# Hybrid decoder step on one core: 22 cache copies moved as quarters behind the input projection's loads, feed-forward job tables rewritten, one tile of the last pair split by halves

## The chip, the cores and the metric

One core of one Trainium2 chip runs the whole program. The metric is the device time in microseconds (us); lower is better. The kernel before was timed three times: 886.66, 887.09 and 891.93 us, median 887.09.

## The reference

One layer of a hybrid decoder, for 512 prompt tokens and 8 sample tokens that share all weights. What it computes, cut to what matters here:

```python
u = rmsnorm(x)
qA,kA,vA, qB,kB,vB,rB,gate, gA,gB = split(u @ w_in)
oA  = dilated window attention (3 groups x 4 heads; for the sample also over the caches)
oB  = gated linear attention (4 heads, state 128 x 256 per head; for the sample a step from state_gla)
mix = sigmoid(gA) * (oA @ w_pa) + sigmoid(gB) * (oB @ w_pb);   h = x + mix @ w_o
y   = rmsnorm(h + square(relu(rmsnorm(h) @ w_up)) @ w_down)
s_aG_k = concatenate(cache_aG_k, new k)[-window:]     # likewise v, for the groups G = 1, 2, 3
```

The last line matters for the change: the caches of the sample group are outputs, each shifted by one token. The bulk of them is nothing but a copy from DRAM to DRAM, 42 MB in all: 1 MB for each of a1k and a1v, 4 MB for each of a2k and a2v, 16 MB for each of a3k and a3v.

## The kernel before, in words

**Data.** The 520 token columns (512 + 8) are worked in two halves of 260. Every float32 operand is split into a high part (rounded to fp32r) and a low part (the rest), so each weight tile of 128x128 costs three products on PE: high x high, high x low and low x high. Weights come in panels of 128 output columns. A panel of 512 KB is loaded by SP (`load`, the DMA is at L118; each such DMA is chained behind the one before), its high half is made by ACT (`act`, L159) and its low half by DVE (`add`, L162; the three-operand form is at L165).

**Order of the panels.** 58 panels of the input projection (three groups of kA, qA, vA; then rB; then for each of the four GLA heads kB, qB, vB; then the gates gA and gB), then w_pa, w_pb and w_o, all in a plain loop over k tiles (`panel_mms`, products at L304); panel i+2 is loaded while panel i is multiplied. Between the products of these panels stand the small steps of attention and GLA. One of these chains recurs below, once per GLA head: SP writes a small tile `dV` (L1060, 8 KB), loads it back spread out as `sx<-dV` (L1072), ACT scales it (L1086), further steps give `ov` (ACT, L1092), and PE multiplies that into `gsp` (L1097) in its fixed place among the products. All these DMAs stand in SP's one queue, together with the panel loads and with `sx<-in_state` (L1071).

**The feed-forward.** Four quarters of it, each with four pairs of w_up panels and, in the first three, four pairs of w_down panels: 28 pairs. A pair multiplies two panels at once with seven groups of 12 products in place of eight, P1 to P7 (`pair_mm`, L262), on sums of activations (T, f) and sums of weights. A sum of weights is built by a plain load of one tile and, on the POOL queue, a DMA that adds another tile to it (`load_sums`, L146); DVE adds a further raw tile into `s`. The table `PLAN` has one line per pair that sets the order on all three engines by hand: P1 to P7 are the products, s, h and l followed by a number are the weight jobs (a sum on DVE, the high part on ACT, the low part on DVE), letters such as t2, f2, rt, sf, st, c0, hT, lT, ht, lt are the steps on the activations; "+" means for the next pair and "-" for the one before. After the last pair, the last eight w_down panels run in a plain loop (L1545 to L1575, products at L1562) in two column halves, 280 then 240. For each panel of it SP loads a tile `h` of the residual; in the first half `h` is added on DVE for the first four panels, and from the fifth panel on ACT writes it into PSUM ahead of the products (`mps<-h`, L1559), behind the splits `lw` of the next panel.

**The copies.** `pace` (L344 to L353, the DMA is at L349) issues one 1 MB copy from POOL's queue when PE has reached the last product recorded. All 42 copies go this way: 18 between the end of the gate projections (404 us) and the start of the feed-forward, 21 behind the products P4 of pairs, one more behind P4 of the last pair, and the rest in the last loop's first half, where `pace` is called after its fourth panel and later.

**Where the copies are called in the feed-forward**

```python
if p == "P4":
    self.pace(banks["copies"])
...
b = {"copies": k % 2 or qd == 3}     # up pairs
b = {"copies": 1}                    # down pairs
```

Of the kernel before, what the change touches and what calls it, by code (L numbers as in the profile page):

```python
# [13 lines left out]
ALU = mybir.AluOpType  # L14
# [25 lines left out]
l1 h7 -x0 l7 l5 P1 -y0 -y1 P5 ca h3 h4 l3 P6 u1 l4 h2 l2 P3 +X u2 +s1 +h5 -u5 P7 +h6 -u6 +l6 P2 u3 +h1 +l5 u4 P4  # L40
l1 s2 P1 h7 h3 h2 l3 P5 ca l2 -x0 -u6 -y0 P6 u1 l7 h4 -x1 l4 P3 u2 -y1 -u5 +h1 +s1 P7 +h6 P2 u3 +h5 +s2 u4 +h3 P4
l1 h7 l3 -u5 -x0 l5 P1 h2 l6 +s1 P5 ca -y0 +h1 +l1 P6 k5 l2 -x1 l7 h4 P3 k6 -y1 -u6 +s2 l4 P7 +h6 f2 +h3 rf2 P2 t2 sf2 +l6 +h5 +l3 rt2 P4
-rf1 l5 -st2 h7 +s1 -sf1 P1 -c0 -rt1 -c3 -st1 -c1 -ht1 l7 P5 -hf1 ca +s2 h2 -lf1 -hT1 -lt1 P6 k5 -c2 h4 l2 -hT0 -lT1 P3 k6 l4 -ht2 -hT2 +h1 -lT2 P7 -lT0 +h6 -lt2 +l1 +h3 P2 t2 +h5 f2 rt2 +l3 rf2 st2 P4
# [35 lines left out]
class Build:  # L79
# [163 lines left out]
    def pair_mm(self, plan):  # L243
# [10 lines left out]
        for t in plan.split():  # L254
            n = t.lstrip("+-")
            if n[0] == "P":
# [9 lines left out]
                if p == "P4":  # L266
                    self.pace(banks["copies"])
# [9 lines left out]
    def panel_mms(self, xh, xl, m, pool=None):  # L277
# [1473 lines left out]
```

## Time and profile before

| what | value |
|---|---|
| timed runs, median of 3 | 887.09 us (886.66 to 891.93) |
| the profiled execution: its own time | 882.92 us |
| its span, first to last instruction | 880.7 us |
| PE busy (products) | 862.4 us, 98% of the span |
| DVE, ACT, POOL busy | 660.3, 484.7, 111.7 us |
| mean granted TensorE clock | 0.995 |
| DMA queues q1 (SP) and q0 (POOL) | 35.0% and 28.3% of 16 engines' span |

How to read it: the profiled execution lies 4.17 us below the median of the timed runs, and 2.2 us of its time lie outside its span. A line number is that of the kernel printed above. "idle before" is the time in which an engine waited directly ahead of an instruction, and the arrow names what ended the wait. The granted clock of 1.00 is TensorE's upper level (2.4 GHz), 0.50 its lower (1.2 GHz). The DMA share is the mean busy share of the core's 16 DMA engines; it can read above 1 where two queues' packets overlap in time.

### The profile page before, as it was taken

Reading aid. Unit: us, or ns where it says so; the run is one execution under the profiler, and the core shown is the slowest. Engines: PE = TensorE matmul, PEld = TensorE weight load, DVE = VectorE, ACT = ScalarE, POOL = GpSimd, SP = SyncE. Lnnn points to the kernel's source line nnn. Section 1 sums busy time; section 2 is a strip of 40 time slices with the busy share of each in tenths; the row PEclk is TensorE's granted clock in tenths of the full one; section 3 lists DMA queues with packets and bytes.
Section 4 is the critical chain, followed back from the end, with each engine's and each line's share of the span. In section 5 each row is a group of like instructions: output and inputs, shape, how many; then the busy total and the mean of one; then the engine's idle time right before and its main releaser. Section 6 shows DMA issues by size and latency. Waiting matters only on the chain.

```text
span 880.7 us, 19661 instructions
## 1 busy us (share of the span) xinstructions
PE 862.4 (98%) x7818; PEld 843.7 (96%) x7818; DVE 660.3 (75%) x1377; ACT 484.7 (55%) x1062; POOL 111.7 (13%) x163
## 2 busy tenths in 40 slices
PE   8999999999999999999999999999999999999896
PEld 8999999999999999999999999999999999999795
DVE  6867576776866959686855678986998999988743
ACT  7243423462635536354733457976894598458543
POOL 1111000001111212111000120111111111120000
PEclk9999999999999999999999999999999999999998
DMA  7476455334445354224599896899698879887732
GB/s 260 118 277 197 146 199 186 114 114 128 150 163 197 122 185 145 86 77 170 198 362 337 313 329 174 255 282 348 187 287 264 257 221 271 267 264 231 273 123 82
DMA packets 53474, 184.13 MB, mean 209 GB/s; under 512 B 6716, under 2 KB 13892, under 8 KB 51560
## 3 DMA queue, kind: packets, MB, share of 16 engines
q1 hardware_dynamic: 39736, 106.39, 35.0%
q0 software_dynamic: 13360, 76.01, 28.3%
q8 instruction: 61, 1.00, 0.4%
q10 hardware_dynamic: 288, 0.49, 0.2%
q14 instruction: 29, 0.24, 0.1%
HBM read 167.01 MB, written 56.30 MB: 254 GB/s over the span
## 4 chain that ended last, share of the span: by engine, by line
PE 90%; DMA 4%; DVE 3%; issue 1%; ACT 1%; SPq 0%; DVEq 0%; ACTq 0%
PE mps L304 48%; PE mps L262 28%; PE mps L1562 4%; DMA sums<-in_w_up 2%; PE mps L470 1%; PE sps L645 1%; PE lev L899 1%; PE pvp L678 1%; PE gpo L1008 1%; PE gpu L1012 1%; PE ptp L662 1%; PE vps L609 1%; DMA xr<-in_xT 1%; PE gpo L1010 1%; DMA h<-Hd 1%
## 5 line engine op out<-in xcount | busy, mean ns | idle before, releaser
L304 PE MATMUL mps<-uh,whi 128*128 128x260 f32 x896 | 255.8, 286 | 0.0
L304 PE MATMUL mps<-ul,whi 128*128 128x260 f32 x896 | 255.7, 285 | 0.0
L304 PE MATMUL mps<-uh,wlo 128*128 128x260 f32 x896 | 255.2, 285 | 0.0
L159 ACT ACTIVATE whi<-raw 128x512 fp32r<-128x512 f32 (+1 forms) x210 | 129.1, 619 | 184.6 <-PE mps L304 150.4
L162 DVE TENSOR_TENSOR wlo<-raw,whi 128x512 fp32r<-128x512 f32 (+1 forms) x210 | 141.3, 677 | 44.9 <-ACT whi L159 43.2
L304 PEld LDWEIGHTS mps<-uh,wlo 128*128 128x128 f32 x896 | 168.7, 188 | 2.1 <-issue 1.5
L304 PEld LDWEIGHTS mps<-ul,whi 128*128 128x128 f32 x896 | 168.7, 188 | 1.2 <-issue 0.3
L304 PEld LDWEIGHTS mps<-uh,whi 128*128 128x128 f32 x896 | 168.7, 188 | 1.1 <-issue 0.7
L262 PE MATMUL mps<-Th,wlo 128*128 128x260 f32 x256 | 72.3, 282 | 1.7 <-DVE wlo L162 1.7
L262 PE MATMUL mps<-Tl,whi 128*128 128x260 f32 x256 | 72.2, 282 | 0.3 <-DVE Tl L162 0.3
L262 PE MATMUL mps<-Th,whi 128*128 128x260 f32 x256 | 72.3, 283 | 0.0
L262 PE MATMUL mps<-hh,wlo 128*128 128x260 f32 x240 | 67.8, 283 | 0.5 <-DVE wlo L162 0.5
L262 PE MATMUL mps<-hl,whi 128*128 128x260 f32 x240 | 67.8, 282 | 0.0
L262 PE MATMUL mps<-hh,whi 128*128 128x260 f32 x240 | 67.6, 282 | 0.0
L262 PE MATMUL mps<-fh,whi 128*128 128x260 f32 x192 | 54.5, 284 | 0.4 <-DVE dd L162 0.4
L262 PE MATMUL mps<-fh,wlo 128*128 128x260 f32 x192 | 54.1, 282 | 0.0
L262 PE MATMUL mps<-fl,whi 128*128 128x260 f32 x192 | 54.0, 281 | 0.0
L1562 PE MATMUL mps<-fh,lw 128*128 128x280 f32 (+1 forms) x256 | 49.0, 291 | 3.6 <-ACT mps L1559 3.2
L159 ACT ACTIVATE whi<-s 128x512 fp32r<-128x512 f32 x56 | 34.3, 624 | 31.4 <-DVE s L162 16.4
L262 PEld LDWEIGHTS mps<-Th,wlo 128*128 128x128 f32 x256 | 48.2, 188 | 1.9 <-DVE wlo L162 1.9
L262 PEld LDWEIGHTS mps<-Tl,whi 128*128 128x128 f32 x256 | 48.2, 188 | 0.5 <-DVE Tl L162 0.5
L262 PEld LDWEIGHTS mps<-Th,whi 128*128 128x128 f32 x256 | 48.2, 188 | 0.1
(386 smaller groups left out, 2154.9 us busy)
## 6 DMA issues: line engine op xcount, KB each, us to landing
raw<-in_w_in SPq DMA_DIRECT2D x55, 512.0 KB, 4.5
raw<-in_w_down SPq DMA_DIRECT2D x20, 512.0 KB, 6.9
sums<-in_w_up SPq DMA_DIRECT2D x16, 512.0 KB, 5.9
sums<-in_w_up POOLq DMA_DIRECT2D x16, 512.0 KB, 6.6
raw<-in_w_up SPq DMA_DIRECT2D x16, 512.0 KB, 6.6
sums<-in_w_down SPq DMA_DIRECT2D x12, 512.0 KB, 5.0
sums<-in_w_down POOLq DMA_DIRECT2D x12, 512.0 KB, 6.0
sx<-in_state SPq DMA_DIRECT2D x8, 512.0 KB, 4.6
```

The costliest lines, as they stand in the source:

```text
L159: return self.turn("ACT", self.nc.scalar.activation(*args, **kw))
L162: return self.turn("DVE", self.nc.vector.tensor_tensor(out, a, b, op=op))
L262: mm = nc.tensor.matmul(into.get(p, x), w[:, k], u, start=(p in ("P1", "P5") and k == 0 and y == 0), stop=(k == 3 and y == 2), skip_group_ ...
L304: mm = self.nc.tensor.matmul(o[:, :HC], wt, x[:, k, j * HC:(j + 1) * HC], start=(k == 0 and n == 0), stop=(k == kt - 1 and n == 2))
L470: self.last = nc.tensor.matmul(ps[i][:, j, :HC], wt, u[:, k, j * HC:(j + 1) * HC], start=(k == 0 and n == 0), stop=(k == KT - 1 and n == 1))
L609: nc.tensor.transpose(pt[:, r * P:(r + 1) * P], vt[:, r * P:(r + 1) * P], self.c["ident"])
L645: m = nc.tensor.matmul(pss[hh][:, hp, c], Q[rows, i, b * P:(b + 1) * P], K[rows, i, ks], start=True, stop=True)
L662: nc.tensor.transpose(pt[:, hh, x], prs[hp][:, hh, x * P:(x + 1) * P], self.c["ident"])
L678: m = nc.tensor.matmul(po[64 * hh:64 * hh + 64, hp * P:(hp + 1) * P], v, pTs[hp][:, hh, x], start=(x == first), stop=(x == 1))
L899: m = self.nc.tensor.matmul(out, w, x, start=True, stop=True)
L1008: nc.tensor.matmul(po[:, :256], ST[:, c], V[:, c], start=True, stop=(c == 0))
L1562: self.last = nc.tensor.matmul(ps, w, u[:, kk, cc], start=(early and kk == 0 and x == 0), stop=(kk == KT - 1 and x == 2), skip_group_check ...
```

## The change

1. **The copies.** The last 22 copies of the list (all 16 of a3v, 6 of a3k) are cut into four quarters of 16 rows x 16 KB, 88 DMAs of 256 KB. From panel 10 of the input projection on, two quarters follow each panel load on SP's queue (L118). The calls of `pace` at P4 are gone. The other 20 copies stay on POOL: 18 at their places before the feed-forward, and two at the first two calls of `pace` in the last loop, after its fourth and fifth panel.
2. **PLAN.** All 28 lines are rewritten. What is multiplied stays; the order of the jobs of ACT and DVE differs nearly everywhere. In the first line PE's order changes too: P1 P5 P2.01 P6 P3 P7 P2.23 P4 becomes P1 P5 P6.012 P2.01 P3.0 P6.3 P3.123 P7 P2.23 P4 (the digits behind a point are k tiles).
3. **The last pair.** The tile f (sf, vf, hf, lf: square, scaling, high part, low part) is worked by column halves of 260 in place of 520, and hp4 and lp4, the split of the second half of the first last-loop panel, stand together ahead of P3.

The instructions that PE, DVE, ACT, POOL and SP issue change by 0, +2, +2, -22 and +88.

```diff
             else:
...
-                if p == "P4":
-                    self.pace(banks["copies"])
...
         if i + 2 < len(self.panels):
             self.load_panel(i + 2)
+        for q in self.quarters[:2] if i >= 10 else ():
+            self.load(*self.quarters.pop(0))
...
-        for n, z, x in (("f", f, 0), ("t", t, 4)):
-            jobs["s" + n] = func(z, z, AF.Square)
-            jobs["v" + n] = lambda z=z: self.add(z(), z(), rv, op=ALU.mult)
-            jobs.update(parts(n, z, *tile(x, everything)))
+            for h, cc in (("", everything), ("1", one), ("2", two)):
+                i = of(z, cc)
+                jobs["s" + n + h] = func(i, i, AF.Square)
+                jobs["v" + n + h] = lambda i=i, cc=cc: self.add(i(), i(), rv[:, cc], op=ALU.mult)
+                jobs.update(parts(n + h, i, *tile(x, cc)))
...
+        self.quarters = []
+        for o, i in (self.copies.pop() for x in range(22)):
+            self.quarters += [[t[:, y * t.shape[1] // 4:(y + 1) * t.shape[1] // 4] for t in (o, i)] for y in range(4)]
...
-                    b = {"copies": k % 2 or qd == 3}
+                    b = {}
...
-                    b = {"copies": 1}
+                    b = {}
```

The last line of PLAN, as an example of the table:

```diff
-h5 -rf1 l5 -sf P1 h7 -vf -hf P5 ca -lf +hp0 l3 -rt1 -rt2 P6 k5 l7 -st l4 h2 +lp0 P3 k6 -vt +hp4 l2 -ht P7 R -lt P2 t2 f2 g2 rf2 q2 P4 rf1 +lp4 ht2 sf lt2 vf g1 hf q1 lf ht1 lt1
+l5 -rf1 h4 l4 P1 h7 l3 -sf -rt1 -vf P5 ca l7 -hf +hp0 -lf P6 k5 +lp0 +hp4 -st +lp4 P3 k6 -vt h2 -ht l2 P7 R f2 -lt rf2 sf2 P2 t2 vf2 g2 hf2 q2 P4 rf1 lf2 ht2 sf1 lt2 vf1 g1 hf1 q1 lf1 ht1 lt1
```

SP's queue around the third GLA head of the sample step: the last panel loads ahead of the write of `dV`, its reading back, the next panel load and the load of the state. Before:

```order
L118 DMA raw<-in_w_in 128x1024 x4
L1060 DMA dV<-vs 8x256
L1072 DMA sx<-dV 128x1024 x2
L118 DMA raw<-in_w_in 128x1024
L1071 DMA sx<-in_state 128x4x256 x2
```

And now:

```order
L118 DMA raw<-in_w_in 128x1024
L118 DMA out_ca3v<-in_ca3v 16x4096 x2
L1060 DMA dV<-vs 8x256
L1072 DMA sx<-dV 128x1024 x2
L118 DMA raw<-in_w_in 128x1024
L118 DMA out_ca3k<-in_ca3k 16x4096 x2
L1071 DMA sx<-in_state 128x4x256 x2
```

The sequence of the old DMAs is the same; two quarters now stand directly ahead of `dV`, and two more between the next panel load and the load of the state. `sx<-dV` follows `dV` directly, as before.

DVE's queue at the end of the last pair, with the numbers of the tiles (lw is a low weight part of the first last-loop panel, P5 and P6 are parts of products that ACT has copied out, mps the PSUM banks, t the tiles from which f comes, fl the low part of f). Before:

```order
L162 TENSOR_TENSOR wlo_11057<-raw_10707,whi_11056 128x512
L162 TENSOR_TENSOR fl_7067<-t_10970,fh_7066 128x520
L162 TENSOR_TENSOR t_11107<-mps_10997,P5_11051 128x260
L162 TENSOR_TENSOR t_11109<-mps_10995,P6_11072 128x260
L165 SCALAR_TENSOR_TENSOR t_11111<-t_11107,acc_6485 128x260
L165 SCALAR_TENSOR_TENSOR t_11107<-t_11107,t_11111 128x260
L162 TENSOR_TENSOR lw_10992<-raw_10851,lw_10991 128x512
L162 TENSOR_TENSOR fl_7067<-t_11107,fh_7066 128x260
L162 TENSOR_TENSOR t_11109<-t_11109,acc_6485 128x520
L165 SCALAR_TENSOR_TENSOR t_11111<-mps_10997,acc_6485 128x260
L165 SCALAR_TENSOR_TENSOR t_11107<-mps_10997,t_11111 128x260
L162 TENSOR_TENSOR fl_7067<-t_11109,fh_7066 128x520
```

And now, from the split of that panel on:

```order
L162 TENSOR_TENSOR lw_11060<-raw_10918,lw_11059 128x512 x2
L162 TENSOR_TENSOR t_11037<-t_11037,acc_6573 128x520
L162 TENSOR_TENSOR wlo_11142<-raw_10780,whi_11141 128x512
L162 TENSOR_TENSOR t_11162<-mps_11063,P6_11138 128x260
L162 TENSOR_TENSOR fl_7155<-t_11037,fh_7154 128x520
L162 TENSOR_TENSOR t_11179<-mps_11065,P5_11120 128x260
L162 TENSOR_TENSOR t_11162<-t_11162,acc_6573 128x260
L165 SCALAR_TENSOR_TENSOR t_11182<-t_11179,acc_6573 128x260
L165 SCALAR_TENSOR_TENSOR t_11179<-t_11179,t_11182 128x260
L162 TENSOR_TENSOR fl_7155<-t_11162,fh_7154 128x260
L162 TENSOR_TENSOR fl_7155<-t_11179,fh_7154 128x260
L162 TENSOR_TENSOR t_11162<-t_11162,acc_6573 128x260
```

Both halves of the split `lw` stand seven instructions and more ahead of where the second one stood, the scaling of f (`t<-t,acc`, 520 wide before) is two instructions of 260, the first of them ahead of the part that waits for the last products, and `fl` of f follows by halves as well. Behind these rows the last loop's instructions keep their order on DVE, ACT and SP.

## Rows read from the trace of the kernel before

**Rows 1.** What PE waited for, over the whole span: line waited for, us in total, times, longest us. The lines left out belong to stages that the change does not touch.

```profile
PE mps L1562 <- ACT mps L1559: 3.2, 1, 3.2
PE mps L262 <- DVE wlo L162: 2.2, 2, 1.7
...
PE gsp L1097 <- ACT ov L1092: 0.5, 1, 0.5
PE mps L262 <- DVE dd L162: 0.4, 1, 0.4
PE mps L1562 <- ACT fh L159: 0.4, 1, 0.4
PE mps L1562 <- DVE fl L162: 0.3, 1, 0.3
PE mps L262 <- DVE Tl L162: 0.3, 1, 0.3
```

**Rows 2.** Stretches of the span by windows: window, length, busy us (and instructions) of PE, PE's weight loads, DVE, ACT and POOL, then the granted clock, the DMA share and GB/s.

```profile
80.00:430.00 350.00, 349.47 (x3586) 336.07 (x3585) 244.14 (x575) 164.92 (x375) 41.48 (x63) 1.00 0.44 148
606.00:621.00 15.00, 12.85 (x106) 12.44 (x105) 9.29 (x17) 8.72 (x19) 2.96 (x3) 1.00 0.99 309
621.00:806.00 185.00, 184.49 (x1539) 184.09 (x1538) 170.97 (x337) 131.74 (x296) 27.96 (x31) 1.00 0.86 258
```

**Rows 3.** POOL's timeline from 597 to 622 us: start, length, line, operation, tiles; in brackets the idle time before and what ended it.

```profile
600.03 1.21 POOL L146 DMA_DIRECT2D sums<-in_w_up  x1 [7.20 <-DVE dd L162]
602.35 0.52 POOL L349 DMA_DIRECT2D out_ca3k<-in_ca3k  x1 [1.11 <-PE mps L262]
606.84 1.22 POOL L146 DMA_DIRECT2D sums<-in_w_up  x1 [3.97 <-ACT dd L159]
```

**Rows 4.** The timelines of DVE and PE from 609.5 to 621 us, same columns.

```profile
610.04 0.69 DVE L162 TENSOR_TENSOR s<-sums,raw 128x512 f32<-128x512 f32 x1 [2.83 <-DMA sums<-in_w_up]
...
617.33 0.69 DVE L162 TENSOR_TENSOR s<-sums,raw 128x512 f32<-128x512 f32 x1 [2.88 <-issue]
...
620.49 0.39 PE L262 MATMUL mps<-Th,wlo 128*128 128x260 f32 x1 [1.70 <-DVE wlo L162]
```

**Rows 5.** The DMA issues of the profile page: tiles, queue, count, size of one, median us from issue to landing.

```profile
raw<-in_w_in SPq DMA_DIRECT2D x55, 512.0 KB, 4.5
...
sums<-in_w_up POOLq DMA_DIRECT2D x16, 512.0 KB, 6.6
```

**Rows 6.** The same view of the window 599 to 608 us alone.

```profile
sums<-in_w_up POOLq DMA_DIRECT2D x2, 512.0 KB, 10.2
...
out_ca3k<-in_ca3k POOLq DMA_DIRECT2D x1, 10.2
```

**Rows 7.** The same view of the whole span: the 16 copies of a3v.

```profile
out_ca3v<-in_ca3v POOLq DMA_DIRECT2D x16, 7.6
```

**Rows 8.** POOL's timeline ahead of the third late weight, and PE's row that it ended.

```profile
776.47 1.20 POOL L146 DMA_DIRECT2D sums<-in_w_up  x1 [4.68 <-DVE wlo L162]
777.21 1.00 POOL L349 DMA_DIRECT2D out_ca3v<-in_ca3v  x1
...
784.41 0.39 PE L262 MATMUL mps<-hh,wlo 128*128 128x260 f32 x1 [0.51 <-DVE wlo L162]
```

**Rows 9.** The timelines of ACT and DVE at the last pair's end.

```profile
819.44 0.64 ACT L159 ACTIVATE fh<-t 128x520 fp32r<-128x520 f32 x1 [0.77 <-DVE t L162]
...
820.12 1.03 DVE L162 TENSOR_TENSOR fl<-t,fh 128x520 fp32r<-128x520 f32 x2
```

**Rows 10.** The timelines of SP, DVE and ACT behind it, to the long wait: the residual tile and the load that the chain goes through.

```profile
822.98 2.67 SPq L118 DMA_DIRECT2D h<-Hd  x1
...
827.88 0.45 DVE L162 TENSOR_TENSOR dd<-dd,h 128x280 f32<-128x280 f32 x1 [1.52 <-DMA h<-Hd]
...
829.56 0.33 SPq L118 DMA_DIRECT2D raw<-in_w_down  x1
...
832.99 1.15 ACT L159 ACTIVATE lw<-raw 128x512 fp32r<-128x512 f32 x2 [2.06 <-DMA raw<-in_w_down]
834.04 0.39 ACT L1559 ACTIVATE mps<-h 128x280 f32<-128x280 f32 x1
```

**Rows 11.** Windows as in rows 2: 819 to 823 us, and two equal stretches behind the long wait.

```profile
819.00:823.00 4.00, 3.25 (x22) 2.67 (x21) 3.90 (x9) 3.39 (x7) 0.49 (x1) 1.00 1.22 485
...
835.20:838.60 3.40, 3.40 (x17) 3.40 (x16) 2.84 (x6) 1.09 (x3) 0.00 (x0) 0.50 0.39 81
838.60:842.00 3.40, 3.40 (x28) 3.40 (x28) 1.26 (x3) 1.36 (x4) 0.49 (x1) 1.00 1.01 354
```

**Rows 12.** What ACT waited for between 200 and 345 us (the four GLA heads), columns as in rows 1.

```profile
ACT whi L159 <- DMA raw<-in_w_in: 7.7, 3, 3.0
ACT sx L1086 <- DMA sx<-dV: 7.3, 4, 3.0
```

**Rows 13.** The timelines of SP, ACT and PE at the third head.

```profile
297.93 0.29 SPq L1060 DMA_DIRECT2D dV<-vs  x1
299.64 1.68 SPq L1072 DMA_DIRECT2D sx<-dV  x2
...
304.19 0.51 ACT L1086 ACTIVATE sx<-sx,kqs 128x256 f32<-128x256 f32 x1 [2.01 <-DMA sx<-dV]
...
306.96 0.66 PE L1097 MATMUL gsp<-ident,ov 128*128 128x128 f32 x4 [0.53 <-ACT ov L1092]
```

More of the change, by code (lines that the diff above doesn't have):

```diff
@@ L40 @@
[L40 to L43, printed above, removed]
@@ new lines @@
+h7 l6 h3 l5 P1 l3 +s1 P5 ca h2 l2 P6 u1 l7 -x0 h4 -y1 P3 +X u2 +h1 +l1 P7 +h6 l4 -u6 +s2 x0 P2 u3 +h3 -u5 +l3 +h5 P4
+--u4 h7 l6 l5 P1 h2 +s1 l7 l2 P5 ca -u6 -y0 h4 P6 u1 +h1 +l1 P3 +X u2 +s2 -x1 -y1 P7 +h6 l4 -u5 -u4 P2 u3 +h5 +h3 +l5 x0 +l6 P4
+h7 l7 P1 h2 l3 -u4 l2 P5 ca +s1 -y0 +s2 P6 u1 h4 P3 u2 -x1 -y1 P7 +h6 l4 +h5 P2 u3 +h1 +l5 -u6 x1 +l1 P4
+--u5 l6 h3 -x0 -u5 P1 -y0 l3 -y1 P5 ca h7 h2 l7 P6 k5 +s1 h4 l2 P3 k6 +s2 -u6 l4 +h1 -u4 P7 +h6 f2 rf2 +l6 +h3 P2 t2 +h5 rt2 +l5 sf2 st2 +l1 P4
+h7 -c0 -rf1 l3 -ht2 P1 -lt2 -rt1 +s1 -sf1 -st1 -hf1 +s2 P5 ca -c1 h4 -lf1 l7 h2 P6 k5 -c2 -ht1 -c3 +h1 l2 P3 k6 -lt1 l4 -hT2 -hT0 -hT1 -lT0 P7 f2 +h6 -lT2 rf2 -lT1 +h3 P2 t2 +h5 +l1 rt2 sf2 +l3 P4
@@ new lines @@
+-rf1 l6 -st2 -c0 -ht2 -sf1 l5 P1 -rt1 -lt2 h7 -c1 -st1 -c3 P5 ca +s1 -hT0 l7 h2 -c2 -hf1 P6 k5 +s2 -ht1 -lT0 -hT2 -lf1 h4 P3 k6 -lT2 -lt1 +h1 l4 -hT1 l2 P7 +h6 f2 -lT1 +h3 P2 t2 +h5 +l1 rt2 rf2 +l3 st2 P4
+h7 l6 -ht2 l5 -sf2 -rf1 P1 -c0 -rt1 l7 -sf1 +h1 -c1 -st1 -c3 P5 ca -c2 -ht1 +l1 h4 +s1 P6 k5 -lt2 h2 -lt1 -hf1 l2 -hT2 P3 k6 l4 -hT0 -hT1 -lT2 -lf1 P7 +h6 f2 -lT1 rf2 -lT0 sf2 P2 t2 +h5 +s2 rt2 st2 +l5 P4
+-rf1 -sf1 -hf1 -c0 -c3 -lf1 P1 -hT0 -c1 -lT0 h3 -hT1 l6 P5 ca -lT1 -rt1 h7 l3 -st1 P6 u1 -ht2 -lt2 h2 l7 -ht1 h4 P3 u2 +h5 l2 -c2 P7 l4 -hT2 -lT2 -lt1 P2 u3 +h1 +s1 +l1 P4
@@ new lines @@
+h7 s2 h6 l5 P1 l6 h2 h3 l3 P5 ca -u4 l7 P6 u1 +h1 h4 +l1 P3 u2 l4 l2 P7 +s1 -u5 +h6 P2 u3 +h5 +s2 -u6 +h3 P4 Z
+l6 h7 -u4 l5 P1 -z l7 z0 P5 ca h2 l3 h4 P6 u1 +s1 P3 u2 -u6 l4 P7 l2 +h6 +s2 +h1 P2 u3 +h5 +l5 +l1 P4
+h7 -u4 h3 --u5 l6 P1 l3 l7 P5 ca -z1 h2 -u5 h4 P6 u1 +h1 l2 P3 u2 +s1 z0 P7 l4 -u6 P2 u3 +h5 u4 +l1 P4
+l5 h7 -u5 l7 P1 h2 s2 h6 l2 l6 P5 ca h3 h4 l3 P6 k5 +s1 -z1 P3 k6 +h5 +s2 l4 P7 +h6 +l5 +h3 +l6 P2 t2 +h1 f2 rt2 -u6 st2 +l1 P4
+-rf2 -rf1 l3 -sf2 -sf1 -c0 h7 P1 +s1 -rt1 -c1 -st1 l7 h2 P5 ca l2 -ht2 -hT1 -lt2 P6 k5 -lT1 h4 -c2 -c3 -hT2 +s2 P3 k6 +h1 -lT2 l4 -hT0 -hf1 P7 f2 -ht1 +h6 -lT0 -lf1 rf2 -lt1 P2 t2 sf2 +h5 +l1 +h3 +l5 P4
@@ new lines @@
+-rf1 l6 -rt2 -sf1 l3 -st2 P1 h7 -c0 +s1 -rt1 h4 -c3 -st1 P5 ca +s2 h2 l4 -ht1 -c1 P6 k5 l2 -hf1 l7 -ht2 -hT0 -lf1 P3 k6 -lT0 +h1 -c2 -lt2 -hT1 -lt1 P7 -hT2 f2 +h6 -lT1 +h3 -lT2 P2 t2 rf2 +h5 +l1 rt2 +l3 P4
+-rf1 l6 -st2 -sf2 l5 -sf1 P1 -c0 h7 +s1 -rt1 -c3 -st1 -c1 -hf1 P5 ca +s2 -hT1 l7 h2 P6 k5 -lf1 -c2 h4 -lT1 -hT0 l4 -hT2 P3 k6 -lT0 -ht1 -ht2 l2 +h1 P7 f2 +h6 -lt2 rf2 -lT2 sf2 -lt1 P2 t2 +h5 +l1 rt2 st2 +l5 P4
+-rf1 -sf1 -hf1 -c0 -c3 -lf1 h3 P1 -hT0 -c1 -lT0 -hT1 l6 P5 ca l3 -lT1 h7 -rt1 P6 u1 -st1 -ht1 -ht2 l7 -lt2 h2 P3 u2 h4 -c2 +h1 l2 -hT2 P7 -lt1 -lT2 l4 P2 u3 +h5 +s1 +l1 P4
@@ new lines @@
+h2 -u4 h6 l5 s2 P1 l2 h3 l6 h4 P5 ca -u6 h7 -u5 l3 P6 u1 +h1 l7 -v0 P3 u2 -v1 l4 P7 +s1 u4 +h6 P2 u3 +s2 +l1 +h3 P4
+l6 h5 l5 P1 h7 -u6 l3 -u5 P5 ca l7 h2 -v0 h4 P6 u1 +h5 -v1 P3 u2 +l5 l2 P7 l4 P2 u3 +h1 +l1 +s1 P4
+h6 s2 h7 l6 P1 h2 -u5 h3 l7 P5 ca -u4 l3 -u6 P6 u1 h4 -v0 +h1 -v1 P3 u2 l4 l2 P7 +s1 +l1 P2 u3 +h5 +h6 +l5 +l6 P4
+s2 -u4 h3 P1 h7 l3 h2 -u5 P5 ca l7 h4 -v0 +s1 P6 k5 -u6 +h5 +s2 l4 P3 k6 l2 -v1 P7 +h6 f2 +l5 rf2 +h3 P2 t2 +h1 rt2 +l1 +l3 P4
+h7 l6 -rf1 l7 P1 h2 -sf -rt1 -vf P5 ca +s1 -st -hf P6 k5 -lf +s2 P3 k6 -vt l2 -ht h4 P7 -lt +h6 l4 +h1 f2 P2 t2 +h3 +l1 +h5 +l5 P4
@@ L1224, in up_pair @@
                 jobs["q" + x] = lambda cc=cc, o=o: self.stt(t()[:, cc], o(), 0.0, g()[:, cc], op0=ALU.min, op1=ALU.mult)
-                jobs.update(parts("t" + x, of(t, cc), *tile(4, cc)))
         return jobs
```

29 lines of the change are left out of this document (6 added, 23 removed).

## The prediction

> **What bounds the kernel now.** I read four views in this order: what PE waited for, the windows by stage, the timelines around the few waits, and what ACT waited for in the heads. PE is the bound: it is busy for 98% of the span, and the first view lists every wait of any size that the change can reach. They sum to 3.2 + 2.2 + 0.5 + 0.4 + 0.4 + 0.3 + 0.3 = 7.3 us [rows 1]. The number of products is unchanged, so these 7.3 us and one stretch at the lower clock are all that can be won in the profiled execution; anything beyond must come from what the timed runs have and this execution has not. The windows say where the waits stand: in 80 to 430 us PE is busy for 349.47 of 350 at a DMA share of 0.44, in 606 to 621 us for 12.85 of 15 at a share of 0.99, and in the next 185 us for 184.49 [rows 2].
>
> The waits at 611 and 620 us have one cause in the timelines. POOL issues an accumulate for a sum of weights at 600.03, a copy at 602.35 and the next accumulate at 606.84 [rows 3]. DVE, which needs the sums, stands until 610.04 and again until 617.33, and PE waits 1.70 us for the low part made from them [rows 4]. Those two accumulates took 10.2 us to land against 6.6 in the median of the feed-forward, and the copy beside them also 10.2 against 7.6 [rows 5 to 7]. At 776.47 and 777.21 an accumulate and a copy stand together again, and PE waits 0.51 us at 784.41 [rows 8]. The longest wait, 3.24 us before 834.5, is at the end of a chain: residual tile h (issued 822.98), the addition at 827.88, which waited 1.52 us for it, the splits behind that, the load at 829.56 that needs the freed buffer, its splits at 832.99, and only then the copy of h into PSUM at 834.04, because ACT keeps its order [rows 10]. After it the clock is at 0.50 for 3.4 us [rows 11].
>
> **The change part by part.**
>
> *First pair.* The P6 products of k = 3 move from the 16th place behind P5 to the 19th, three products later; a product starts every 0.12 us (28 in 3.40 us [rows 11]), so the 0.36 us cover the wait of 0.3 for Tl [rows 1]. **-0.3** (0 to -0.3).
>
> *The 21 copies in the feed-forward.* They go from POOL. At 10.2 against 6.6 us the two accumulates would land 3.6 us earlier, more than the 2.83 and 2.88 us that DVE stood [rows 4 to 7], so both of PE's waits there go, and the one at 784 us: 2.2 + 0.4 = 2.6 us [rows 1]. What is late next are the plain loads, which take the same DMA engines; with 21 MB less to move they also come earlier. **-2.6** (0 to -2.6).
>
> *The new order of all 28 lines.* Durations and counts stay, so what can change is when a weight part is ready. The old order lost 0.51 us of 185 beside copies [rows 2, 8]. The trace cannot show the new one. Bounds: nothing lost, or as much as the old order lost at its three places, 2.6 us. I take **+0.7**, nearer to the 0.51 that 17 pairs cost.
>
> *The last pair.* ACT's high part of f begins at 819.44 and takes 0.64, DVE's low part begins at 820.12 and holds DVE for 1.03 together with the next [rows 9]. By halves the first half is squared and scaled 0.2 us each earlier and no 520-wide step remains behind the last products: fl comes some 0.65 us earlier, and PE's waits of 0.4 and 0.3 go [rows 1]. By itself this wins nothing, since PE then only reaches the 3.24 us wait sooner. What counts is the chain to the copy of h. It gains the 0.65 us at its head, for the splits that follow fl free the buffer of the load ahead of h. It gains more where h lands: the copy at 819 is gone, in whose stretch the DMA share was 1.22 [rows 11]; at most the 1.52 us that the addition waited [rows 10]. I take 1.35 of these: **-2.0** together (-0.65 to -2.2). PE arrives 0.6 us earlier, so it still waits 3.24 - 2.0 + 0.6 = 1.85 us there.
>
> *The clock.* At 0.50, 17 products took 3.40 us, at 1.00 28 did [rows 11]; 17 would have taken 2.06, so the fall cost 1.3 us. It followed a wait of 3.24, while behind the wait of 1.70 at 620 us the window reads 1.00 [rows 2, 4]. With 1.85 left I expect no fall: **-1.3** (0 to -1.3).
>
> *The quarters in the input projection.* 88 x 256 KB are 23 MB. At the 354 GB/s of a stretch with a share of 1.01 [rows 11] that is 65 us of all 16 engines; in the 350 us of the window the share goes from 0.44 to about 0.63 [rows 2]: there is room on average. What matters is the queue. One quarter is 0.74 us at that rate and two are 1.5. In the third head two stand directly ahead of dV, whose chain ends in a product that PE already waits 0.53 us for [rows 13]; ACT waits for sx in all four heads, 7.3 us together, and three times for a panel load, 7.7 us [rows 12]. If the two quarters have mostly drained when dV is issued (the load ahead of them is waited for by its buffer, so not always), dV is late by 0 to 1.5 us at the third head. For the other heads no wait of PE's is on record, so I count a small rest. **+0.8** (0 to +3: the 1.5 twice, once at the head and once at a panel load). SP's issue of 88 DMAs at about 0.3 us each [rows 13] lies in its idle time. The two copies left in the last loop keep their places: 0.
>
> The Trainium skill has a rule that speaks against this part (DMA: Bandwidth & Descriptors, section "Queues, rings and completion order"): each DMA engine alternates packet by packet between the queue rows that have work, but takes one row's ring in order. By it a copy on POOL's queue only shares with a panel load, while quarters on SP's queue are to be finished with first; two of them would delay every load and dV issued behind them by up to 1.5 us, and the sum would end at the +3 of this term rather than at +0.8. No row of this trace has a copy ahead of a load in one queue.
>
> *Sum* on the profiled execution: -0.3 - 2.6 + 0.7 - 2.0 - 1.3 + 0.8 = **-4.7**, so 882.92 goes to 878.2. The timed median lies 4.17 us above that execution; with the same distance the forecast is **882.4 us**, 0.5% below 887.09. About 1% is what a measurement of this kernel can tell from no change, that is 878.2 and 896.0.
>
> **The rivals.**
>
> *B, a larger gain.* The 4.17 us that timed runs take beyond the profiled one may themselves be late accumulates and late loads beside copies: the waits here depend on when transfers meet, and one of three runs was 5 us slower still. Then they go with the copies, 882.4 - 4.2 = 878.2, and a chain that is faster throughout takes another 1.2 of the last wait: **877**. For it: the waits are all waits for transfers. Against it: the same distance could lie outside the program, where no edit reaches.
>
> *C, slower.* In SP's queue a quarter may hold up what follows by its share of a copy's 7.6 us [rows 7] rather than by 0.74: 1.9 us, two of them 3.8. The third head has nothing to cover it (PE waits already [rows 13]): +3.8. Two panel loads for which ACT waits 3.0 us already [rows 12] come 3.8 later, and if splits done ahead cover half, PE loses 1.9 twice: +3.8. A wait of 3.8 is longer than the one after which the clock fell: +1.3. Together +8.9 in place of +0.8: **890.5**. It decides as soon as the input projection loses more than the 5.5 us that the other terms win. For it: the place of dV directly behind two quarters. Against it: share 0.44, and loads there land in 4.5 us [rows 2, 5].
>
> *D, it does not do what it says.* The accumulates come late through the loads, not the copies (share 0.86 to 0.99 [rows 2]), or the new order has waits of its own of the same size, and h lands as late as before, so that only -0.3 - 0.65 + 0.8 remain: **886.9**. For it: 21 copies stood among 28 accumulates, and most of these came in time. Against it: the two latest landings were those around one copy.
>
> **How the numbers follow.** The forecast 0.45, B 0.25, D 0.2, C 0.1. The likeliest one's own range runs from all gains and no cost (-0.3 - 2.6 - 2.0 - 1.3 = -6.2, 880.9) to a cost of +3 in the input projection and +2.6 by the order (886.5). The range for 8 in 10 goes from 875, below B, to 889, short of C. Faster by over 1%: most of B and a little of the forecast, 0.27. Slower by over 1%: the worse half of C, 0.05. Within 1%: 0.68.
>
> **What would show it.** Right: PE's waits for wlo and dd in the feed-forward gone or under 1 us together, accumulates without landings near 10 us, the wait for the copy of h at about 1.8 us, no stretch at 0.50 behind it, PE's wait for ov at the third head at 0.5 to 2 us. Wrong: new waits of PE's on panels between 200 and 350 us (C), waits of 2 us and more for wlo at other places of the feed-forward (D), or a profiled execution near 878 with timed runs beside it (B).

## The result, and the profile after

The changed kernel takes 879.13 us in the median of six runs (878.70 to 880.73); the kernel before took 888.76 in the median of six, the three shown ahead and three more (886.66 to 891.93). The ratio is 0.989 with a 95% interval of 0.9865 to 0.9914: some 1.1% faster, at the edge of what can be told apart, and inside the forecast range of 875 to 889. The forecast was 882.4.

The profiled execution took 878.73 us, its span is 876.9. That is 4.2 us below the profiled one of before, while the timed medians differ by 9.6: the first thing to explain is why the timed runs won twice as much.

The waits of PE in the changed kernel, over the whole span, same columns as [rows 1]:

```profile
PE mps L1566 <- ACT mps L1563: 3.0, 2, 2.3
...
PE mps L1566 <- DVE fl L162: 0.8, 1, 0.8
```

The lines left out are of the first 20 us and the very end, and one of 0.2 us. The waits for wlo, dd, Tl, fh and ov of [rows 1] are gone; what is left of the 7.3 us is the last loop's. The windows, as in [rows 2]:

```profile
80.00:430.00 350.00, 349.96 (x3583) 335.87 (x3582) 243.53 (x574) 162.42 (x373) 42.15 (x63) 1.00 0.61 213
606.00:621.00 15.00, 15.00 (x128) 15.00 (x127) 10.84 (x20) 11.64 (x26) 1.19 (x1) 1.00 0.78 190
621.00:806.00 185.00, 185.00 (x1547) 184.88 (x1546) 171.79 (x336) 131.79 (x298) 20.30 (x17) 1.00 0.66 175
```

PE is without a gap in the feed-forward; the DMA share went from 0.44 to 0.61 in the input projection and from 0.86 to 0.66 in the feed-forward. The timeline of POOL answers to [rows 3]: the accumulates stand alone, ten us apart.

```profile
604.77 1.20 POOL L146 DMA_DIRECT2D sums<-in_w_up  x1 [8.22 <-DVE wlo L162]
614.69 1.19 POOL L146 DMA_DIRECT2D sums<-in_w_up  x1 [8.72 <-DVE acc L162]
```

The last loop, timelines of SP, DVE and ACT, answers to [rows 10]:

```profile
820.47 1.35 SPq L118 DMA_DIRECT2D h<-Hd  x1
...
824.28 0.45 DVE L162 TENSOR_TENSOR dd<-dd,h 128x280 f32<-128x280 f32 x1 [0.42 <-DMA h<-Hd]
...
825.97 0.33 SPq L118 DMA_DIRECT2D raw<-in_w_down  x1
...
829.58 1.15 ACT L159 ACTIVATE lw<-raw 128x512 fp32r<-128x512 f32 x2 [2.14 <-DMA raw<-in_w_down]
830.63 0.39 ACT L1563 ACTIVATE mps<-h 128x280 f32<-128x280 f32 x1
```

h lands 3.8 us after its issue in place of 4.9, but the load at 825.97 needs 3.6 (3.4 before), and ACT is behind it once more. The window behind the wait that ends at 831.07 is at the upper level of the clock (columns as in [rows 2]):

```profile
831.07:834.16 3.09, 3.09 (x24) 3.09 (x24) 3.09 (x6) 0.39 (x1) 0.00 (x0) 1.00 0.39 131
```

What ACT waited for in the four heads, as in [rows 12]:

```profile
ACT sx L1086 <- DMA sx<-dV: 10.6, 4, 4.3
ACT whi L159 <- DMA raw<-in_w_in: 8.0, 3, 3.8
```

These waits grew by 3.3 and 0.3 us; between 80 and 435 us the waits for panel loads grew from 7.7 to 15.5 us. PE's product for the third head no longer waits for ov all the same, since the write of dV moved little (297.79 after a pair of quarters issued at 295.22) and sx landed 0.5 us sooner.

PE's position at five points shows where the time went (starts of its products in the two profiled executions, us):

| point | before | after | difference |
|---|---|---|---|
| first product of the plain loop | 18.61 | 18.58 | -0.03 |
| first product of the feed-forward | 530.94 | 531.94 | +1.01 |
| first product of the last pair | 807.21 | 804.25 | -2.97 |
| last product of the feed-forward | 818.56 | 816.50 | -2.06 |
| end of PE | 872.57 | 868.57 | -3.99 |

The row of the last product of the feed-forward hides 0.9 us of the gain, and the section on the change lacks what hides it: PE's order has changed in the last pair too. Products of the last loop stand among those of the last pair, 11 of them before and 18 now. The windows of the last pair for the last loop's products alone (window, length, busy us and number of PE and of its weight loads, granted clock, DMA share, GB/s), first before and then now:

```profile
807.21:818.65 11.44, 1.74 (x11) 1.60 (x12) 1.00 0.62 212
```

```profile
804.25:816.60 12.35, 2.82 (x18) 2.47 (x18) 1.00 0.42 140
```

With the PLAN of before it is 11 with the copies moved as well (experiment 2), with the new one 18 with the copies on POOL as well (experiment 3). So the feed-forward is better measured up to the first product of its last pair: it went from 276.3 to 272.3 us. From there to the end of PE it was 65.4 us and is 64.3.

### The profile page after: what moved, and what is told of

It is laid out like the page before. It is cut to its first block, busy times and chain, and to the rows that moved or that the text cites. A ratio compares the mean times of both kernels' runs of the same rounds, so it can differ in the third digit from the quotient of the medians.

```text
span 876.9 us, 19715 instructions
## 1 busy us (share of the span) xinstructions
PE 861.9 (98%) x7818; PEld 841.9 (96%) x7818; DVE 660.8 (75%) x1379; ACT 483.9 (55%) x1064; POOL 100.6 (11%) x141
## 4 chain that ended last, share of the span: by engine, by line
PE 95%; DMA 2%; ACT 1%; DVE 1%; issue 1%; SPq 0%; DVEq 0%
PE mps L304 48%; PE mps L262 32%; PE mps L1566 4%; PE lev L899 1%; PE mps L470 1%; PE sps L645 1%; PE pvp L678 1%; DMA h<-Hd 1%; PE gpo L1008 1%; PE gpu L1012 1%; PE ptp L662 1%; PE vps L609 1%; DMA raw<-in_w_in 1%; PE gpo L1010 1%; DVE lw L162 1%
## 5 line engine op out<-in xcount | busy, mean ns | idle before, releaser
L162 DVE TENSOR_TENSOR wlo<-raw,whi 128x512 fp32r<-128x512 f32 (+1 forms) x210 | 143.4, 685 | 56.2 <-ACT whi L159 52.6
L262 PEld LDWEIGHTS mps<-hh,wlo 128*128 128x128 f32 x240 | 45.2, 188 | 0.0
```

The costliest lines, as they stand in the source:

```text
L162: return self.turn("DVE", self.nc.vector.tensor_tensor(out, a, b, op=op))
L262: mm = nc.tensor.matmul(into.get(p, x), w[:, k], u, start=(p in ("P1", "P5") and k == 0 and y == 0), stop=(k == 3 and y == 2), skip_group_ ...
```

## The experiments

Each is timed against the kernel before on the same chip (medians of 11 to 28 runs of it: 886.97, 889.09 and 887.36 us). An experiment's own runs are 6 to 12. The changed kernel's 879.13 was not timed beside them, so where an experiment is set against it and differs by 1 to 2 us, the lengths of the stages in the two profiles say more than the medians.

**1. The kernel before, again.** No edit.

> The kernel before, once more, as a measure of its own spread. My theory (the timed runs of before lose more than the profiled one at the same places, because the accumulates and the copies meet at different moments): its timed runs spread over some 5 us, 886 to 892, and a second profile shows PE's waits for wlo, dd and the copy of h at more than the first one's 2.2, 0.4 and 3.2 us, with a span of 884 to 889. Rival (the distance of 4 to 6 us between the profiled execution and the timed ones lies outside the program): the second profile has the same waits within 0.5 us and a span of 880 to 881, while the timed runs stay at 887 to 891.

Measured: 886.32 us (883.10 to 894.09), ratio 0.999 (0.9959 to 1.0025). Over all runs of this kernel its time lies between 882.0 and 895.5, so the first profile, with 882.92, was one of its best executions. The second profile took 892.22, and its waits are larger at the same kind of place, but for wlo's (1.3 in place of 2.2):

```profile
PE mps L1562 <- ACT mps L1559: 5.9, 1, 5.9
PE mps L262 <- ACT P L159: 3.3, 1, 3.3
PE mps L262 <- DVE dd L162: 2.7, 1, 2.7
PE mps L262 <- DVE wlo L162: 1.3, 1, 1.3
```

The wait of 3.3 us begins with an accumulate issued at 709.07 that landed after 9.4 us. DVE stands for it, its timeline shows, and ACT for DVE, and PE for a tile `P` that stands behind on ACT, which copies it out of PSUM:

```profile
718.52 0.69 DVE L162 TENSOR_TENSOR s<-sums,raw 128x512 f32<-128x512 f32 x1 [4.35 <-DMA sums<-in_w_up]
```

None of the cache copies was under way beside this accumulate. POOL's timeline around it has one at 697.94, directly behind an accumulate that landed after 5.5 us, and the next at 715.82, which moved no packet before 718.44:

```profile
697.94 1.00 POOL L349 DMA_DIRECT2D out_ca3v<-in_ca3v  x1
709.07 1.21 POOL L146 DMA_DIRECT2D sums<-in_w_up  x1 [10.13 <-DVE fl L162]
715.11 1.19 POOL L146 DMA_DIRECT2D sums<-in_w_down  x1 [4.83 <-DMA sums<-in_w_down]
715.82 1.01 POOL L349 DMA_DIRECT2D out_ca3v<-in_ca3v  x1
```

What did run beside it were the plain loads: SP's queue had 48.8% of the 16 engines' time between 709.07 and 718.44. The two profiles of before have 13 accumulates of over 8 us behind 535 us, and four of these had no packet of a copy beside them. SP's loads had a share of 0.39 and 0.47 of the engines beside the late ones of the two profiles, in the mean, and of 0.11 and 0.09 beside the others. So most late accumulates are those that meet the plain loads, with or without a copy beside them.

Each of the three larger waits is followed by a stretch near the lower level of the clock. The windows behind those that end at 721.46, 776.07 and 843.27 (the second and third run on into a stretch at the upper level):

```profile
721.46:724.00 2.54, 2.54 (x11) 2.54 (x12) 2.54 (x6) 2.40 (x6) 0.00 (x0) 0.50 0.00 0
...
776.00:779.50 3.50, 3.43 (x17) 3.43 (x18) 3.37 (x7) 0.59 (x2) 0.00 (x0) 0.56 1.44 380
...
843.30:848.00 4.70, 4.70 (x22) 4.70 (x23) 0.91 (x2) 1.32 (x3) 0.00 (x0) 0.57 0.25 67
```

So the distance between the profiled and the timed runs lies in the program: other executions of the same kernel have more and longer late weights, the longest with a fall of the clock behind them. My theory held in the main (the spread of 11 us and the second span of 889.8 are wider than I had expected), and rival B's first half with it.

**2. Only the copies.** The changed kernel with the PLAN of before (and so the last pair unsplit).

```diff
-PLAN of after
+PLAN of before
```

> Only the 22 copies are moved, as quarters on SP's queue; PLAN and the last pair as before. My theory (the copies beside the accumulates make the late weights): 0.990 to 0.993 of before, timed runs close together, the waits for wlo and dd in the feed-forward gone, the wait for Tl of 0.3 us in the first pair still there, the wait for the copy of h 2.5 to 3.2 us. Rival (the new order of the jobs makes the gain): 0.997 to 1.003, with waits for wlo of 2 us and more.

Measured: 880.62 us (879.13 to 882.05), 0.993 (0.9897 to 0.9964). In its profile the feed-forward takes 273.4 us up to the first product of the last pair, against 272.3 in the changed kernel, 276.3 and 283.7 in the two profiles of before. The wait of 0.3 for Tl is there, one of 0.3 for wlo is left, the wait for the copy of h is 2.2. The copies alone bring most of the gain, as my theory had it; with them moved, the new order is worth 1.1 us more in the feed-forward. Two things I had not expected. PE waits once for 1.7 us in the input projection, for a DVE that has worked without a pause since a late `sx<-dV` (ACT waited 4.4 us for it); from the plain loop's first product to that of the feed-forward it takes 515.8 us, against 513.4 in the changed kernel. And two of the three accumulates issued between 598 and 618 us took 9.4 and 9.0 us, though no copy is left in the feed-forward (the median of the three stands last):

```profile
sums<-in_w_up POOLq DMA_DIRECT2D x3, 512.0 KB, 9.0
```

So an accumulate can be late without a copy near it. In the changed kernel, without copies there and with the new order, none takes over 7.7 us.

**3. Only PLAN and the halves.** All 42 copies paced on POOL.

```diff
-        for q in self.quarters[:2] if i >= 10 else ():
-            self.load(*self.quarters.pop(0))
...
+                if p == "P4":
+                    self.pace(banks["copies"])
```

> The new PLAN and the last pair by halves, with all 42 copies on POOL as before. My theory: the accumulates still land late beside copies, so 0.997 to 1.003 of before, waits for wlo and dd of 1.5 us and more in the feed-forward, spread of the timed runs as in before. Rival (the new order makes the gain): 0.989 to 0.993, waits in the feed-forward under 0.5 us.

Measured: 891.63 us (886.02 to 897.11), 1.004 (1.0006 to 1.0071). Waits of 4.7 us for P, 2.9 for dd and 6.4 for the copy of h; the feed-forward takes 282.7 us up to the last pair. The new order by itself is worth nothing while the copies are where they were, and is if anything worse.

**4. Without the 22 copies.**

```diff
+        self.quarters = []
```

> The changed kernel with the 22 copies left out (all of a3v and 6 MB of a3k are not written), so neither POOL nor SP carries them. It prices the quarters in the input projection. My theory (quarters delay dV and loads a little): 1 to 1.5 us less than the changed kernel, 0.987 to 0.989 of before; the last product of the plain loop over panels at 530.8 us as in before or 0.6 us earlier, against 531.8 in the changed kernel. Rival (the 1 us is the order of the small products on PE, not the quarters' traffic): that product stays at 531.5 to 532 and the time within 0.3 us of the changed kernel.

Measured: 877.24 us (876.16 to 878.16), 0.988 (0.9839 to 0.9922). From the first product of the plain loop to that of the feed-forward it takes 511.7 us, against 513.4 in the changed kernel and 512.3 before: the quarters cost 1.6 us there, and the timed medians differ by 1.9. The feed-forward takes the same as with the copies moved. Over all kept profiles that stage takes 511.5 to 512.4 us in the nine without the 22 copies in it and 513.1 to 515.8 in the five with them, so their price varies between executions.

**5. The quarters on POOL's queue in the input projection.**

```diff
-            self.load(*self.quarters.pop(0))
+            o, x = self.quarters.pop(0)
+            c = self.nc.gpsimd.dma_start(o, x)
...
+                self.after(c, self.last)
```

> The changed kernel with its 88 quarters issued from POOL's queue in place of SP's, at the same panels. My theory (on SP's queue the loads and dV stand behind the quarters): ACT's waits for sx<-dV fall from 10.6 us in the changed kernel back to 7 to 8 as in before, those for panel loads from 15.5 to 8 to 12, and the time is 0.5 to 1.5 us below the changed kernel, 0.987 to 0.989 of before. Rival (what costs is the share of the 16 engines, whatever the queue): the same waits within 1 us and the same time, 0.989. A second rival: POOL, which needs some 0.5 to 1 us for each issue, becomes late with its own transposing and writing steps, and the time goes above 0.991.

Measured: 878.81 us (878.00 to 881.13), 0.9895 (0.9862 to 0.9927): no difference in time. What ACT waited for between 80 and 435 us:

```profile
ACT whi L159 <- DMA raw<-in_w_in: 16.2, 4, 5.0
ACT sx L1089 <- DMA sx<-dV: 9.8, 4, 4.2
```

In the changed kernel the same lines are 15.5 and 10.6 over this window, without the quarters (experiment 4) 8.8 and 8.0. My theory, that loads and dV pay for standing behind the quarters in one queue, fell; the first rival, the share of the engines, fits. The second, a late POOL, did not happen: PE's one new wait, 1.4 us for `state`, stands behind a split whose panel load ACT waited 5.0 us for.

**6. The quarters in the feed-forward, on SP's queue.**

```diff
-        for q in self.quarters[:2] if i >= 10 else ():
-            self.load(*self.quarters.pop(0))
...
         self.load_panel(i + 2)
+        for q in self.quarters[:4 if i % 7 == 0 else 3]:
+            self.load(*self.quarters.pop(0))
         e = banks["e"]
```

> The changed kernel with the 88 quarters behind the loads of the 28 pairs of the feed-forward, on SP's queue, three for a pair and four times four; none in the input projection. It keeps the bytes in the feed-forward but takes them off POOL's queue, where the accumulates are. My theory (bytes in the feed-forward are the cause: 22 MB more there leave the 16 engines too little slack): waits of PE's in the feed-forward of 3 us and more come back, 0.995 to 1.003 of before. Rival (the accumulates are late because they share POOL's queue with the copies): no waits there over 1 us, 0.987 to 0.990, about 1.5 us better than the changed kernel as the input projection is free of quarters.

Measured: 877.38 us (876.34 to 877.78), 0.987 (0.9838 to 0.9906). The whole feed-forward by windows, first here and then in the kernel before:

```profile
531.00:806.00 275.00, 275.00 (x2297) 274.70 (x2296) 251.24 (x487) 206.14 (x469) 30.27 (x26) 1.00 0.89 263
```

```profile
531.00:806.00 275.00, 272.03 (x2263) 271.00 (x2263) 246.62 (x480) 202.65 (x458) 41.45 (x46) 1.00 0.85 259
```

More bytes pass here than before, at a DMA share of 0.89, and PE has no gap. The theory that bytes in the feed-forward were the cause fell; POOL's queue, the size of a piece or its place were left.

**7. The copies whole on SP's queue in the input projection**, one behind every second panel load.

```diff
-            self.quarters += [[t[:, y * t.shape[1] // 4: ...
+        self.quarters = [self.copies.pop() for x in range(22)]
...
+        for q in self.quarters[:1] if i >= 10 and i % 2 == 0 else ():
```

> The changed kernel with the 22 copies whole, 1 MB each, on SP's queue behind every second panel load from panel 10 on: the same bytes in the same stretch in four times larger pieces. My theory (a load behind a piece waits for the piece, so its size is what it costs): 1 MB is 3 us of all engines, so ACT's waits for panel loads and sx<-dV grow from 26 to 35 us or more, PE loses 2 to 5 us in the input projection, 0.992 to 0.995 of before. Rival (only bytes count): 0.989 as the changed kernel.

Measured: 878.65 us (877.76 to 882.33), 0.9896 (0.9862 to 0.993). ACT's two waits are 13.2 and 8.7 us, less than with quarters. The size of a piece made no difference there; cutting the copies brought nothing.

**8 to 10. Queue against size in the feed-forward.** The whole copies on SP behind the loads of 22 pairs; the quarters on POOL at the pairs' starts; the whole copies on POOL at the same starts.

```diff
+        for q in self.quarters[:1] if (i + 1) * 22 // 28 > i * 22 // 28 else ():
+            self.load(*self.quarters.pop(0))                       # 8
...
+        for q in self.quarters[:4 if i % 7 == 0 else 3]:           # 9; 10 with the line above
+            o, x = self.quarters.pop(0)
+            c = self.nc.gpsimd.dma_start(o, x)
...
+                self.after(c, self.last)
...
```

> The changed kernel with the 22 copies whole, on SP's queue behind the loads of 22 of the 28 pairs of the feed-forward; the quarters there had cost nothing. First of three that separate queue and size in the feed-forward. Theory Q (POOL's queue is to blame: an accumulate shares it with a copy and lands late): no wait of PE's over 1 us in the feed-forward, accumulates over 8 us at most two of 28 there, 0.986 to 0.989 of before. Theory S (size is to blame: 1 MB in one piece holds up what meets it): waits of 3 us and more, 0.994 to 1.002.

> The changed kernel with the 88 quarters on POOL's queue in the feed-forward, three or four at the start of each pair behind the loads and the accumulate issued there. Theory Q: waits of 3 us and more in the feed-forward, 0.994 to 1.003 of before. Theory S: no waits over 1 us, 0.986 to 0.989.

> The changed kernel with the 22 copies whole, on POOL's queue at the start of 22 of the 28 pairs, in place of behind P4 of them as in before. Theories Q and S both: waits of 3 us and more, 0.994 to 1.004 of before. Third theory P (the place is to blame: behind P4 a copy falls between the issue of an accumulate and its landing, at the pair's start it stands with the loads): no waits over 1 us, 0.986 to 0.990.

Measured, with experiment 6, as medians in us and ratios:

| in the feed-forward | on SP's queue | on POOL's queue |
|---|---|---|
| quarters | 877.38, 0.987 (0.9838 to 0.9906) | 890.77, 1.006 (1.0026 to 1.0089) |
| whole copies | 877.26, 0.9885 (0.9852 to 0.9918) | 888.43, 1.001 (0.9988 to 1.004) |

Neither the size of a piece nor its place among the pairs decides, but whether the copies stand on SP's queue or on POOL's. Up to the last pair the feed-forward takes 272.3 us with either on SP, 284.8 with quarters and 284.2 with whole copies on POOL. On POOL's queue a copy also waits until PE has reached the last product recorded (`self.after`); there, that ended an idle time of POOL's three times with quarters and once with whole copies. The waits of PE in the feed-forward with quarters on POOL (no single one reaches the 3 us that I had expected, together they are 7.8):

```profile
PE mps L269 <- ACT P L159: 5.0, 4, 2.8
PE mps L269 <- DVE t L162: 2.8, 3, 1.4
```

Both kernels on SP have none. How the accumulates fare, from the starts of PE's products and the landings in each trace (the landing of a pair's accumulate against the first product of that pair, from the fifth pair on):

| kernel | copies in the feed-forward | mean latency us | mean landing before use | latest |
|---|---|---|---|---|
| before, two profiles | POOL | 7.0 and 7.1 | 10.6 and 10.9 | 2.6 and 3.1 |
| only PLAN | POOL | 6.8 | 10.2 | 5.1 |
| quarters / whole on POOL | POOL | 7.6 / 7.5 | 9.2 / 9.7 | 5.1 / 4.9 |
| quarters / whole on SP | SP | 6.5 / 7.0 | 11.9 / 10.9 | 10.1 / 8.6 |
| changed; without copies | none | 6.1; 6.1 | 12.5; 12.5 | 9.5; 9.3 |

(The latencies are over the 25 accumulates issued from 535 us on.) The mean latency on SP with whole copies is that of before; what differs is the latest landing. (Three accumulates take over 8 us there, where theory Q allowed two.) With the copies on POOL single accumulates come some 5 us or less before the pair, and DVE and ACT still have to make the splits from them. The plain loads on SP's queue land later as well beside copies on POOL's, most clearly the tile `raw` of the w_up pairs. By the DMA view of 531 to 806 us, its median from issue to landing (the last number, us) is, in the kernel before, with quarters on POOL's queue, with quarters on SP's and in the changed kernel:

```profile
raw<-in_w_up SPq DMA_DIRECT2D x13, 512.0 KB, 6.6
...
raw<-in_w_up SPq DMA_DIRECT2D x13, 512.0 KB, 8.1
...
raw<-in_w_up SPq DMA_DIRECT2D x13, 512.0 KB, 5.7
...
raw<-in_w_up SPq DMA_DIRECT2D x13, 512.0 KB, 5.6
```

How the queue does it stays open. Being under way together is not enough: with quarters, a copy was in flight beside 21 of the 25 accumulates on SP's queue and beside all 25 on POOL's. (With whole copies it was 10 and 24, so there the queue and the meeting in time are not apart.) Whether a late one was held by what stood ahead of it in the ring, by the loads that it met, or was issued late by POOL is not separated: the mean issue is also 0.7 to 1.8 us later than in the changed kernel (0.75 with whole copies on SP).

**11. h earlier in the last loop.**

```diff
+                    if j == 0 and k == 2:
+                        for y in (3, 4):
+                            hs[y] = self.late.tile([P, 4, P], F32, tag="rb", name="hb", bufs=2)...[:, :n]
+                            self.load(hs[y], Hd[:, y, cc])
```

> The changed kernel with the residual tiles h of the fourth and fifth panel of the last loop loaded two panels earlier, ahead of a panel load that waits for its buffer, into the two buffers of a tile that the last pair has done with. My theory (the wait that is left before the fifth panel, 2.3 us, and the 0.7 behind it come from h standing behind that load in SP's queue): both waits gone or under 0.6 us together, 2 to 3 us less than the changed kernel, 0.986 to 0.987 of before. Rival (the chain goes through the panel load itself and its splits): the wait turns into one for lw of the same size, gain under 0.7 us.

Measured: 875.90 us (874.70 to 876.50), 0.985 (0.9822 to 0.9885), 3.2 below the changed kernel. Both waits for the copy of h are gone: ACT now does it at 824.40, ahead of the splits that wait for the last load.

```profile
824.40 0.39 ACT L1570 ACTIVATE mps<-hb 128x280 f32<-128x280 f32 x1
...
830.53 1.15 ACT L159 ACTIVATE lw<-raw 128x512 fp32r<-128x512 f32 x2 [3.36 <-DMA raw<-in_w_down]
```

ACT waits 3.4 us for the load, and nobody waits for ACT.

**12. Experiments 6 and 11 together.**

> The two best parts together: quarters behind the loads of the feed-forward's pairs on SP's queue, and the residual tiles h of the fourth and fifth panel loaded earlier. If the two gains add up (1.7 and 3.2 us of the changed kernel's 879.1): 873.5 to 875, 0.982 to 0.984 of before, and no wait of PE's over 1 us behind the first 20 us. If the quarters in the feed-forward cost the loads of the last loop something: 875 to 876.5.

Measured: 873.12 us (872.85 to 875.54), 0.984 (0.9809 to 0.9876): the best version, 6 us below the changed kernel. The gains of 1.7 and 3.2 add up and 1 us more. Its waits of PE over the whole span:

```profile
PE rps L523 <- DVE eps L432: 1.1, 1, 1.1
PE mps L1573 <- DVE fl L162: 0.8, 1, 0.8
PE r L1596 <- ACT t L1595: 0.3, 1, 0.3
```

## Why the prediction was right, and where not

*First pair, -0.3.* Right. The wait for Tl is gone and reappears when only PLAN goes back (experiment 2).

*The copies in the feed-forward, -2.6.* Too small for the profiled execution: up to the last pair the feed-forward went from 276.3 to 272.3 us, by 4.0, and 0.4 of it lie in the first pair. The waits of [rows 1] there sum to 2.9; that PE lost 1.1 more with them than the view counts as waiting, I had not seen, and why is not shown. The copies alone bring 2.9 (experiment 2). Wrong in what makes it. I put it down to the bytes beside the accumulates; experiments 6 and 8 put as many bytes there at a share of 0.89 and lose nothing, 9 and 10 put them back on POOL's queue and lose all of it. It is the queue that the copies stand in; by what path it makes accumulates late is open.

*The new order, +0.7.* It cost nothing here: no wait of PE's in the feed-forward, and with the copies moved 1.1 us less than the old order, the 0.4 of the first pair among them. I had priced it apart from the copies; experiment 3 shows that the two are not independent, since with copies on POOL the new order is no better than the old one.

*The last pair and the chain to h, -2.0.* This term failed. The landing of h came out about as forecast: 3.8 us after its issue in place of 4.9, a gain of 1.1 in place of 1.35. The gain at the head did not come. Behind the last product of the pair fl came 0.4 us earlier with the halves, but seven more products of the last loop stand ahead of that product and make it 0.9 later. So, from the first product of the last pair, h was issued 0.45 us later than before, where 0.65 earlier was forecast; the load behind it took 0.2 longer, and the copy of h won 0.45 us in all. In experiment 2, with the last pair unsplit, it won 1.0. PE waited 2.3 us, not 1.85, and 0.7 again before the next panel, which I had not seen. The waits for fh and fl, 0.7 together, became one of 0.8 for fl.

*The clock, -1.3.* No fall came behind the 2.3 us, as forecast, but that was luck. In the 14 kept profiles the clock fell behind every wait of PE's of 2.7 us and more and behind none under 2.2; of the ten between, it fell behind six (2.2, 2.2, 2.3, 2.4, 2.5 and 2.6) and not behind four (2.3, 2.4, 2.4 and 2.5). The same wait for the copy of h in experiments 2 and 6, each with the window behind it:

```profile
PE mps L1566 <- ACT mps L1563: 2.2, 1, 2.2
...
834.42:837.83 3.41, 3.41 (x17) 3.41 (x16) 2.06 (x4) 1.26 (x3) 0.00 (x0) 0.50 0.31 84
```

```profile
PE mps L1566 <- ACT mps L1563: 3.4, 2, 2.5
...
828.86:832.27 3.41, 3.37 (x24) 3.14 (x24) 3.28 (x7) 0.66 (x2) 0.00 (x0) 1.00 0.21 42
```

What decides between them is not shown.

*The quarters in the input projection, +0.8.* Measured +1.03 for the stage, net of the wait for ov, which is gone in this profile (0.5 and 0.7 us of it are there in experiments 2 and 11); the quarters themselves cost 1.6 (experiment 4), in other profiles up to 4. What I took for the cause, two quarters ahead of dV in SP's queue, is not: on POOL's queue they cost the same (experiment 5). With it falls the step from the rule of the Trainium skill (DMA: Bandwidth & Descriptors, "Queues, rings and completion order"), by which loads would pay for the pieces ahead of them in their ring, to the +3 of this term. No run shows that here: ACT's waits for loads are 15.5 us with the quarters on SP's queue and 16.2 on POOL's.

*From the profiled execution to the median.* This is the step that failed for the time: I carried the distance of 4.17 us over unchanged. It was not a constant outside the program but the spread of late weights, 882 to 895 us in the kernel before, and it went with the copies: the changed kernel's runs lie within 2 us, its median 0.4 above its profile. The median won 9.6 against a forecast of 4.7.

*The sum.* The sum on the profiled execution, -4.7, met -4.2, but by errors that cancel. The feed-forward up to its last pair won 4.0 where -0.3 - 2.6 + 0.7 = -2.2 was forecast, the last pair and the last loop 1.0 where 3.3 was.

*The rivals.* B had this mechanism, and the result lies nearer to its 877 than to 882.4; its second half, 1.2 us more off the last wait, did not happen. C did not occur, and its cause (a piece holding up what stands behind) is refuted by experiment 7, where pieces of 1 MB on SP's queue cost no more. D's sum is refuted by experiment 2, since the waits went with the copies. Its cause holds in part: what the late accumulates met were loads.

## What to carry to other kernels

When timed runs lie above the profiled one and spread by more than a per cent, look for a transfer that the order on the engines leaves a few us of slack, and profile a second execution: the profile at hand may be the good one (8 of some 80 runs of this kernel were faster than its first profile). Before moving bulk copies to another stage, move them to another queue: here 22 MB in the busiest stage cost nothing once they stood on SP's queue in place of POOL's, though PE depends on loads in SP's as well. When a job is split to come earlier, look at what its being ready early moves ahead on PE. And a short load that stands in one queue behind a load waiting for its buffer should go ahead of it.

## What the runs showed of the hardware that I had not expected

A DMA share of 0.89 over 275 us left all loads of 512 KB in time (experiments 6 and 8). In the feed-forward it mattered in which queue the copies stood, and not only for transfers of that queue. Beside copies on POOL's queue, accumulates landed as late as 2.6 us before use, and the loads of `raw` for the w_up pairs, on SP's queue, took 6.6 to 8.1 us in the median of a profile; with the same bytes between the loads on SP's own queue these took 5.5 and 5.7, and PE never waited in the feed-forward. In the input projection the queue made no difference. And one late transfer can be paid for twice: behind a wait of 2.7 us and more, and behind some from 2.2 us on, the clock stood at its lower level for 3.4 us (6.8 about the two longest waits); 3.4 us at that level pass 17 products in place of 28.
